# An earlier place for evacuations and a shorter lead for weight splits in the Strassen pairs of a hybrid decoder layer

## The chip, the cores and the metric

The kernel runs on 1 core of one Trainium2 chip. The metric is the device time of one execution in microseconds (us). TensorE (PE) multiplies, VectorE (DVE) and ScalarE (ACT) do elementwise work, GpSimd (POOL) helps them, and SyncE (SP) issues all transfers from one in-order queue. Each engine takes its instructions strictly in the order in which the program lists them.

## The reference

One step of a decoder layer for 512 prompt tokens and 8 x 8 sample tokens (576 columns together), with d_model 2048: a norm, one input projection, sparse attention and a gated recurrence side by side, and the merged output. The part that the change touches is the last line:

```python
m = jax.nn.sigmoid(gm_att) * u_att + jax.nn.sigmoid(gm_rnn) * u_rnn
return x + jnp.einsum('btd,de->bte', m, w_out)      # w_out is 2048 x 2048
```

All of it is float32. The kernel holds each operand of a product as a high part (rounded to the type float32r) and a low part (the rest), and adds three matmuls: high x high, high x low and low x high.

## The kernel before

The program is written as a list of *slots*. A slot is the work of one weight block of 128 x 1024 numbers with 288 columns: 24 matmuls (8 row blocks, three each). The main loop (L1502) walks over the slots and writes, for each, in this order: the high parts that are due, transfers and helpers that were put on this slot (`later`), the low parts that are due, the evacuations of the products that ended in the slot before (`evs`), helpers that were put at the slot's end (`behind`), and then the slot's matmuls. As each engine keeps the order in which its own instructions were written, this sets what stands in front of what on VectorE.

The *weight blocks* are split by `w_high` (L220, on ScalarE, tile whi) and `w_low` (L227, on VectorE, tile wlo = block minus high part). The list `wunits` has the slot in which each split is due. There are three buffers for whi and three for wlo (WHL = 3, L207). A split can thus start only when the product three blocks earlier has read its weights for the last time.

The output projection comes last. Its first four row tiles (kind "y") are plain: four slots each, evacuated by L557. While they run, `y_factors` (L1354) makes the sums of the token factors that the Strassen form needs. The other twelve row tiles are done as six *pairs* (kind "Y") by a Strassen scheme of seven products each instead of eight; a product is one slot. For a pair, four blocks of w_out are loaded (tiles yr, three buffers, and ya, two) and four sums of blocks are made from them on VectorE by `y_sum`: the first s1 = a21 + a22 (L1380), then s2 = s1 - a11 (L1384), a21 = a11 - a21 (L1387) and a11 = a12 - s2 (L1390). The last two write over the block that they read. Blocks of products 0 to 6 are: a11, the fourth sum, a12, the third sum, s2, s1, a22. So the high part of product 1 needs the fourth sum, which needs the second, which needs the first, and the fourth sum may only be made when product 0's block has been split.

The products go to PSUM banks by this table (row operand, column half, bank, whether it begins the bank):

```python
YPROD = ((0, 0, "g", True), (1, 1, "s", True), (1, 0, "g", False), (3, 1, "h", True),
         (2, 1, "t", True), (3, 0, "s2", True), (2, 0, "h", False))
```

Product 2 adds into the bank of product 0, and product 6 into that of product 3; g and h are the two banks of the tag "g". Every product is evacuated when it ends (`y_evac`, L1426: the bank times 0.25 is added to one, two or three pieces of the result tile res, 288, 576 or 864 columns). So product 2 may start only when product 0's evacuation is done, since that one must read product 0 alone.

`y_plan` (L1395) puts a pair's loads and sums on slots. With b the pair's first slot: loads on b-7 and b-6, the last of them (a21) at the end of b-6; sums at the end of b-5, b-4, b-3 and b-3. Splits were due three slots ahead of their product.

Of the kernel before, what the change touches and what calls it, by code (L numbers as in the profile page):

```python
# [114 lines left out]
def nsa_rglru_step(ctx, tc, a, o):  # L115
# [68 lines left out]
    slots, wunits, unit_of = [], [], {}  # L184
    for n, (kind, m, units) in enumerate(tiles):
        base = len(slots)
        if n == 0:
            continue
        if kind[0] == "Y":
            for u in range(7):  # L190
                slots.append((n, 0, u))
                unit_of[n, u] = len(wunits)
                wunits.append((n, u, base - 3 + u))
            continue
        for h in range(2):
            for u in range(len(units)):
                slots.append((n, h, u))
        if n == 1:

            slots += [(n, 1, u) for u in (0, 1, 0, 1)]  # L200
            wunits += [(n, 0, -2), (n, 1, -1)]
            continue
        for u in range(len(units)):
            at = base - 2 if len(units) == 1 else (base - 3 if u == 0 else base - 1)
            wunits.append((n, u, at))
# [75 lines left out]
    def square(c):  # L281

        A.activation(xs[c], xs[c], AF.Square)
        if c:
            V.tensor_add(xs[0], xs[0], xs[c])
        if c == 7:
            V.tensor_add(xsum, xs[0][:, 0], xs[0][:, 1])
# [54 lines left out]
    def at(slot, fn, last=False):  # L342

        (behind if last else later).setdefault(slot, []).append(fn)
# [1024 lines left out]
    def y_load(j, c, par_):  # L1369
        tag, bufs = ("ya", 2) if c and par_ else ("yr", 3)  # L1370
        t = rp_["p"].tile([128, 8, 128], F, tag=tag, name=tag, bufs=bufs)
        S.dma_start(t, a["w_out"][j + c, par_])
        yraw[j, c, par_] = t

    def y_sum(n, j, which):

        a11, a21 = yraw[j, 0, 0], yraw[j, 1, 0]
        if which == 1:
            t = ysum[1] = wp.tile([128, 8, 128], F, tag="raw", name="s1", bufs=WRAW)
            V.tensor_add(t, a21, yraw[j, 1, 1])  # L1380
            units = {0: a11, 2: yraw[j, 0, 1], 5: t, 6: yraw[j, 1, 1]}
        elif which == 2:
            t = ysum[2] = wp.tile([128, 8, 128], F, tag="raw", name="s2", bufs=WRAW)
            V.tensor_sub(t, ysum[1], a11)  # L1384
            units = {4: t}
        elif which == 3:
            V.tensor_sub(a21, a11, a21)  # L1387
            units = {3: a21}
        else:
            V.tensor_sub(a11, yraw[j, 0, 1], ysum[2])  # L1390
            units = {1: a11}
        for u, t in units.items():
            raw[unit_of[n, u]] = t

    def y_plan(n, j):  # L1395
        b = slot_of[n]
        at(b - 7, lambda: y_load(j, 0, 0))
        at(b - 6, lambda: (y_load(j, 0, 1), y_load(j, 1, 1)))
        at(b - 6, lambda: y_load(j, 1, 0), True)
        for which, s in ((1, b - 5), (2, b - 4), (3, b - 3), (4, b - 3)):  # L1400
            at(s, lambda which=which: y_sum(n, j, which), True)

    ybank = {}
# [43 lines left out]
    evs = []  # L1447
# [45 lines left out]
    def sample_work(s):  # L1493
        nonlocal sample_n
        while sample_n is not None and sample_n < (s + 0.5 - sample_from) / (sample_to - sample_from):
            sample_n = next(ssteps, None)
# [5 lines left out]
    for s, (n, h, u) in enumerate(slots):  # L1502
        now[0] = s
        kind, m, units = tiles[n]
        if s == slot_of[first_r]:
            for _ in psteps:
                pass
            for _ in ssteps:
                pass
            for fs in [later.pop(k) for k in sorted(later) if k < s]:  # L1510
                for f in fs:
                    f()
            att.close()
            cqs.close()
            rp_["h"] = ctx.enter_context(tc.tile_pool(name="hp", bufs=1))
            rp_["s"] = ExitStack()
            rp_["p"] = rp_["s"].enter_context(tc.tile_pool(name="rp", bufs=1))
            rnn_begin()
        if s == slot_of[first_u] - 9:
            for k in sorted(k for k in later if k <= s):  # L1520
                for f in later.pop(k):
                    f()
            rp_["s"].close()
            rp_["s"] = ExitStack()
            rp_["p"] = rp_["s"].enter_context(tc.tile_pool(name="up", bufs=1))
            for ct in range(8):
                at(s + 3 * ct // 2, lambda ct=ct: oa_make(ct))
        if s == slot_of[first_y]:
            for e in evs:
                evac(*e)  # L1530
            evs.clear()
            rp_["s"].close()
            rp_["p"] = ctx.enter_context(tc.tile_pool(name="yp", bufs=1))
        ws = []
        while wnext < len(wunits) and wunits[wnext][2] <= s:
            w_high(wnext)
            ws.append(wnext)
            wnext += 1
        for f in scales:
            f()  # L1540
        scales.clear()
        for f in later.pop(s, []):
            f()
        if SQS <= s < SQS + 8:
            at(s, lambda c=s - SQS: square(c), True)
        if NORM - 2 <= s < NORM:
            x_mean(s - NORM + 2)
        if s == NORM:
            x_norm()

        if s < slot_of[first_r]:
            if not prompt_done:
                prompt_done = next(psteps, None) is None and s >= sample_from
                if s >= PG and s not in full:
                    at(s, lambda: next(pages, None), True)
                if prompt_done:
                    sample_from = s + 1
                    ssteps = sample_steps()
                    for _ in pages:
                        pass  # L1560
                    pp["stack"].close()
                    pp["s"] = att.enter_context(tc.tile_pool(name="sp", bufs=1))
            else:
                sample_work(s + 0.5)
        for k in ws:
            w_low(k)
            w_load(lnext)
            lnext += 1
        for n2 in range(n, len(tiles)):
            if slot_of[n2] > s + 3:  # L1570
                break
            name, j = tiles[n2][0][0], tiles[n2][0][-1]
            if name in ("ua", "ur") and "p" in rp_ and s >= slot_of[first_u] - 9 and (name == "ur", j) not in gates_in:
                t = gates_in[name == "ur", j] = rp_["p"].tile([128, NT], F, tag="tgi", name="tgi", bufs=4)
                S.dma_start(t, tg_d[int(name == "ur"), j])
            if name in ("y", "Y") and j not in res_in and s >= slot_of[first_y]:
                j -= j % 2
                res_in[j] = res_in[j + 1] = rp_["p"].tile([128, 2, NT], F, tag="res", name="res", bufs=2)
                S.dma_start(res_in[j], xin[j // 2])
        for e in evs:  # L1580
            evac(*e)
        evs = []
        for f in behind.pop(s, []):
            f()

        if n == 1:
            first_products(s)
            continue
        if kind[0] == "Y":
            y_product(n, kind[1], u)  # L1590
            continue
        wh, wl = whl[n, u]
        last = u == len(units) - 1
        for step, (h2, k) in enumerate([(h, k) for k in range(8)]):
            kk = u * 8 + k
            name = kind[0]
            if kk == 0:
                gbs[h2] = bank("g")
            gb = gbs[h2]
            hs = slice(h2 * HF, h2 * HF + HF)  # L1600
            if step == 4 and ssteps is not None and s < slot_of[first_r]:
                sample_work(s + 1)
            if name == "ua":
                r_h, r_l = oa[kk]
            elif name == "ur":
                r_h, r_l = hr[kk]
            elif name == "y":
                r_h, r_l = mh[2 * k + u], ml[2 * k + u]
            else:
                r_h, r_l = xh[kk], xl[kk]  # L1610
            T.matmul(gb[:, :HF], wh[:, k, :], r_h[:, hs], start=kk == 0, stop=False)  # L1611
            T.matmul(gb[:, :HF], wh[:, k, :], r_l[:, hs], start=False, stop=False)  # L1612
            T.matmul(gb[:, :HF], wl[:, k, :], r_h[:, hs], start=False, stop=last and k == 7)  # L1613
            if last and k == 7:
                evs.append((kind, h2, gb))
# [98 lines left out]
```

## Time and profile before

| what | us |
|---|---|
| median of 3 runs | 1746.25 (1742.62 to 1747.58) |
| profiled execution, its own time | 1744.26 |
| its span in the profile | 1742.5 |
| PE busy | 1688.4 (97%) |
| VectorE busy | 1164.6 (67%) |
| ScalarE busy | 824.6 (47%) |

The span is the time from the first instruction to the last; the execution's own time is 1.76 us longer. A row of a timeline has the start, the duration, the engine, the line, the operation, the output and input tiles, the size, and in brackets how long the engine stood idle before it and what ended that. Matmuls are pipelined: a matmul's row is longer (0.29 us) than the distance to the next one, and the distance is what counts. A row of a table of stretches has the stretch, its length, the busy time and count of PE, of the weight loads, of VectorE, ScalarE and GpSimd, and then the granted clock of PE (1.00 is full), the DMA engines' share and GB/s.

### The profile page before, as it was taken

The numbers are of one execution on the slowest core, as the hardware profiler recorded it, in microseconds if no ns is written. First come the engines' busy times: TensorE is split into PE (matmuls) and PEld (weight loads), VectorE is DVE, ScalarE is ACT, GpSimd is POOL, SyncE is SP. The second block draws the span as 40 slices with busy tenths as digits, with TensorE's granted clock in tenths as the row PEclk, the third lists the DMA queues.
The fourth block names the chain that finished last, engine by engine and source line by source line (L and its number), as shares of the span: only waits on it lengthen the run. The fifth ranks groups of instructions, "written<-read, shape, count | busy, mean of one in ns | idle before, by whom it ended". The sixth has DMA issues, their size and how long they took to land. (4 is left out here: it accounts for less than half of the span.)

```text
span 1742.5 us, 33426 instructions
## 1 busy us (share of the span) xinstructions
PE 1688.4 (97%) x12493; PEld 1656.8 (95%) x12493; DVE 1164.6 (67%) x2398; ACT 824.6 (47%) x1521; POOL 473.8 (27%) x503
## 2 busy tenths in 40 slices
PE   9999999999999999999999999999999999997988
PEld 8999989999999899999999999999999999997988
DVE  6578678768778876468777765667664343485655
ACT  6434544553554454367676663666652121232222
POOL 0025435432533344165455520000022111100000
PEclk9999999999999999999999999999999999998999
DMA  6367435433533443466675753222245445463340
GB/s 218 118 214 239 142 99 175 131 106 120 165 101 117 140 156 126 141 191 203 197 207 180 215 171 99 87 79 91 77 159 196 154 146 166 158 237 111 110 151 28
DMA packets 147460, 257.98 MB, mean 148 GB/s; under 512 B 19937, under 2 KB 80482, under 8 KB 147042
## 3 DMA queue, kind: packets, MB, share of 16 engines
q1 hardware_dynamic: 147298, 255.85, 45.7%
q8 instruction: 98, 1.61, 0.4%
q14 instruction: 64, 0.52, 0.1%
HBM read 228.11 MB, written 36.07 MB: 152 GB/s over the span
## 5 line engine op out<-in xcount | busy, mean ns | idle before, releaser
L1611 PE MATMUL g<-xh,whi 128*128 128x288 f32 x2400 | 719.2, 300 | 0.3 <-DVE gm L499 0.2
L1613 PE MATMUL g<-xh,wlo 128*128 128x288 f32 x2400 | 710.0, 296 | 4.5 <-DVE wlo L230 4.5
L1612 PE MATMUL g<-xl,whi 128*128 128x288 f32 x2400 | 709.4, 296 | 0.0
L1613 PEld LDWEIGHTS g<-xh,wlo 128*128 128x128 f32 x2400 | 452.6, 189 | 5.2 <-DVE wlo L230 5.2
L1611 PEld LDWEIGHTS g<-xh,whi 128*128 128x128 f32 x2400 | 453.2, 189 | 2.5 <-DVE gm L499 0.9
L1612 PEld LDWEIGHTS g<-xl,whi 128*128 128x128 f32 x2400 | 453.2, 189 | 1.3
L230 DVE TENSOR_TENSOR wlo<-raw,whi 128x1024 fp32r<-128x1024 f32 x192 | 256.1, 1334 | 44.5 <-ACT whi L224 44.2
L224 ACT ACTIVATE whi<-raw 128x1024 fp32r<-128x1024 f32 x192 | 201.5, 1050 | 60.8 <-PE g L1612 55.5
L851 POOL TENSOR_TENSOR cr<-cr,wcs 128x512 f32<-128x512 f32 x128 | 178.0, 1396 | 151.9 <-DMA cr<-in_cmp 144.1
L703 ACT ACTIVATE p<-p,sm,rq 128x128 f32<-128x128 f32 (+3 forms) x128 | 82.8, 648 | 144.3 <-DVE sm L700 144.2
L960 POOL TENSOR_TENSOR skl<-kr,skh 128x512 fp32r<-128x512 f32 x80 | 114.2, 1431 | 122.5 <-ACT skh L959 83.2
L711 POOL TENSOR_SCALAR p<-p,sm 128x128 f32<-128x128 f32 (+3 forms) x128 | 68.8, 550 | 220.6 <-DVE sm L708 99.4
L722 DVE TENSOR_TENSOR pt<-t,pt 128x512 fp32r<-128x512 f32 x96 | 66.1, 689 | 63.9 <-ACT pt L721 62.6
L1062 DVE TENSOR_TENSOR sv<-vr,sv 128x256 fp32r<-128x256 f32 (+1 forms) x120 | 77.3, 671 | 17.5 <-ACT sv L1058 17.2
L857 DVE TENSOR_REDUCE skvx<-cr 128x16 f32<-128x512 f32 x128 | 86.6, 676 | 0.4
L552 ACT ACTIVATE mh<-ur 128x288 fp32r<-128x288 f32 x32 | 14.2, 445 | 145.0 <-POOL ur L546 145.0
L1613 PE MATMUL g<-oah,wlo 128*128 128x288 f32 x256 | 75.5, 295 | 0.0
L1613 PE MATMUL g<-hrh,wlo 128*128 128x288 f32 x256 | 75.4, 295 | 0.0
L1612 PE MATMUL g<-oal,whi 128*128 128x288 f32 x256 | 75.4, 295 | 0.0
L1611 PE MATMUL g<-oah,whi 128*128 128x288 f32 x256 | 75.4, 294 | 0.0
L1612 PE MATMUL g<-hrl,whi 128*128 128x288 f32 x256 | 75.3, 294 | 0.0
L1611 PE MATMUL g<-hrh,whi 128*128 128x288 f32 x256 | 75.3, 294 | 0.0
(374 smaller groups left out, 3409.2 us busy)
## 6 DMA issues: line engine op xcount, KB each, us to landing
raw<-in_w_in SPq DMA_DIRECT2D x152, 512.0 KB, 3.4
cr<-in_cmp SPq DMA_DIRECT2D x128, 256.0 KB, 3.6
kr<-in_selk SPq DMA_DIRECT2D x128, 128.0 KB, 3.2
vr<-in_selv SPq DMA_DIRECT2D x128, 128.0 KB, 3.1
tg<-gm SPq DMA_DIRECT2D x32, 288.0 KB, 4.4
tgi<-tg SPq DMA_DIRECT2D x32, 288.0 KB, 4.3
yr<-in_w_out SPq DMA_DIRECT2D x18, 512.0 KB, 4.1
raw<-in_w_rnn SPq DMA_DIRECT2D x16, 512.0 KB, 4.1
```

Source lines behind the costliest of these rows:

```text
L224: A.activation(hi, raw[k], AF.Copy)
L230: V.tensor_sub(lo, raw.pop(k), hi.bitcast(F))
L703: A.activation(p[:, :n], p[:, :n], AF.Exp, bias=sm[:, 1, r - r0:r - r0 + 1], scale=rq[:, i, r:r + 1], accum_out=sm[:, 2, r - r0:r - r0 + 1])
L711: G.tensor_scalar(p[:, :n], p[:, :n], sm[:, 3, r - r0:r - r0 + 1], 1.0, op0=OP.mult, op1=OP.mult)
L722: V.tensor_sub(lo, t, hi.bitcast(F))
L851: G.tensor_tensor(v, v, wcs[:, :, None, :].to_broadcast([128, 4, 4, 32]), op=OP.mult)
L857: V.tensor_reduce(x.kvx[:, :, 8 + n * 4:12 + n * 4], v, axis=AX.X, op=OP.add)
L960: G.tensor_tensor(kl, t, kh.bitcast(F), op=OP.subtract)
L1062: V.tensor_sub(v[:, :, :, 1, :], src, v[:, :, :, 0, :].bitcast(F))
L1611: T.matmul(gb[:, :HF], wh[:, k, :], r_h[:, hs], start=kk == 0, stop=False)
L1612: T.matmul(gb[:, :HF], wh[:, k, :], r_l[:, hs], start=False, stop=False)
L1613: T.matmul(gb[:, :HF], wl[:, k, :], r_h[:, hs], start=False, stop=last and k == 7)
```

## The change

In the pairs, the splits are due two slots ahead of their product instead of three; the sums come at the end of b-4, b-3, b-3 and b-2 instead of b-5, b-4, b-3 and b-3; and in the pairs' slots the evacuations are written in front of the low parts instead of behind them. Nothing is computed otherwise, and the loads stay on their slots.

```diff
@@ the list of splits
-                wunits.append((n, u, base - 3 + u))
+                wunits.append((n, u, base - 2 + u))
@@ y_plan
-        for which, s in ((1, b - 5), (2, b - 4), (3, b - 3), (4, b - 3)):
+        for which, s in ((1, b - 4), (2, b - 3), (3, b - 3), (4, b - 2)):
             at(s, lambda which=which: y_sum(n, j, which), True)
@@ the main loop
+        if kind[0] == "Y":
+            for e in evs:
+                evac(*e)
+            evs.clear()
         for k in ws:
             w_low(k)
             w_load(lnext)
```

VectorE's order in the steady state, before: from product 4's evacuation in one pair (from bank t, 864 columns) to product 1's evacuation in the next (from bank s, 288 columns); wlo from yr, s2 or s1 is the low part of the block named, res from g is an evacuation of bank g or h.

```order
L1426 SCALAR_TENSOR_TENSOR res<-t,res 128x864
L230 TENSOR_TENSOR wlo<-yr,whi 128x1024
L1426 SCALAR_TENSOR_TENSOR res<-s,res 128x2x288
L230 TENSOR_TENSOR wlo<-yr,whi 128x1024
L1426 SCALAR_TENSOR_TENSOR res<-g,res 128x288
L230 TENSOR_TENSOR wlo<-s_20643,whi 128x1024
L1426 SCALAR_TENSOR_TENSOR res<-g,res 128x864
L230 TENSOR_TENSOR wlo<-s_20612,whi 128x1024
L1426 SCALAR_TENSOR_TENSOR res<-s,res 128x288
L1380 TENSOR_TENSOR s_20839<-yr,ya 128x1024
```

The evacuation of product 0 (res from g, 864 columns) has the low part of product 4 (from s_20643, the tile s2) directly in front of it. The same stretch of VectorE after the change:

```order
L1426 SCALAR_TENSOR_TENSOR res<-t,res 128x864
L230 TENSOR_TENSOR wlo<-yr,whi 128x1024
L1390 TENSOR_TENSOR yr<-yr,s_20671 128x1024
L1426 SCALAR_TENSOR_TENSOR res<-s,res 128x2x288
L230 TENSOR_TENSOR wlo<-yr,whi 128x1024
L1426 SCALAR_TENSOR_TENSOR res<-g,res 128x288
L230 TENSOR_TENSOR wlo<-yr,whi 128x1024
L1426 SCALAR_TENSOR_TENSOR res<-g,res 128x864
L230 TENSOR_TENSOR wlo<-yr,whi 128x1024
L1426 SCALAR_TENSOR_TENSOR res<-s,res 128x288
L230 TENSOR_TENSOR wlo<-s_20671,whi 128x1024
```

In front of the evacuation of product 0 now stands the low part of product 2 (from yr), and product 4's low part comes after product 1's evacuation. The fourth sum (L1390) stands behind the low part of product 0's block. At the entry into the pairs, VectorE's difference from the last factors (L1366) to the first low parts of the first pair (lines with - are before, with + after):

```order
 L1366 TENSOR_TENSOR tl<-yo,th 128x576
-L230 TENSOR_TENSOR wlo<-yr,whi 128x1024
+L1384 TENSOR_TENSOR s_19767<-s_19725,yr 128x1024
 L1387 TENSOR_TENSOR yr<-yr 128x1024
-L1390 TENSOR_TENSOR yr<-yr,s_19727 128x1024
 L230 TENSOR_TENSOR wlo<-yr,whi 128x1024
 L557 SCALAR_TENSOR_TENSOR res<-g,res 128x288
-L230 TENSOR_TENSOR wlo<-yr,whi 128x1024 x2
+L1390 TENSOR_TENSOR yr<-yr,s_19767 128x1024
+L230 TENSOR_TENSOR wlo<-yr,whi 128x1024
 L557 SCALAR_TENSOR_TENSOR res<-g,res 128x288
```

The first evacuation in this piece (L557, the last plain tile's first half) stood behind the low parts of products 0 and 1 and the fourth sum; it now stands behind the low part of product 0 alone. The first sum (L1380), ahead of this piece, moved from before the last but one set of factors to behind it.

## The prediction

> **What bounds the kernel now.** I read the page first, then TensorE's waits, then a table of stretches over the end of the run, then the timelines of TensorE, VectorE and ScalarE in one pair.
>
> ```profile
> span 1742.5 us, 33426 instructions
> PE 1688.4 (97%) x12493; PEld 1656.8 (95%) x12493; DVE 1164.6 (67%) x2398; ACT 824.6 (47%) x1521; POOL 473.8 (27%) x503
> ```
>
> TensorE (PE) is busy for 97% of the span; everything else has room. So only time in which PE stands still, or runs slowly, can be won. PE's waits from 1300 us to the end (total, times, longest):
>
> ```profile
> PE g L1417 <- DVE res L1426: 20.0, 6, 3.3
> PE g L1417 <- DVE res L557: 4.5, 1, 4.5
> PE g L1611 <- DVE res L557: 1.3, 1, 1.3
> ```
>
> Six waits of 3.3 us, one for each Strassen pair, and one of 4.5 us at the first product: each time the first matmul of a product (L1417) waits until VectorE has evacuated a bank (L1426, L557). The table of stretches has the length, PE's busy time and count, then the other engines, the granted clock and the DMA:
>
> ```profile
> 1526.00:1568.80 42.80, 41.53 (x313) 41.20 (x311) 37.64 (x63) 16.67 (x22) 0.00 (x0) 1.00 0.67 232
> 1568.80:1585.40 16.60, 8.79 (x50) 8.45 (x48) 8.20 (x9) 4.12 (x4) 0.00 (x0) 0.78 0.45 151
> 1639.74:1666.99 27.25, 23.91 (x169) 23.71 (x169) 17.18 (x18) 7.42 (x7) 0.00 (x0) 0.94 0.34 113
> 1694.25:1721.53 27.28, 23.95 (x168) 23.74 (x169) 17.18 (x18) 7.42 (x7) 0.00 (x0) 0.94 0.18 65
> ```
>
> A pair takes 27.25 us, and the clock in it is 0.94, not the 1.00 of the stretch before. PE's timeline around one wait shows why:
>
> ```profile
> 1633.04 0.30 PE L1417 MATMUL s<-mh,whi 128*128 128x288 f32 x1
> ...
> 1636.11 0.29 PE L1419 MATMUL s<-mh,wlo 128*128 128x288 f32 x1
> 1639.74 0.58 PE L1417 MATMUL g<-mh,whi 128*128 128x288 f32 x1 [3.33 <-DVE res L1426]
> 1640.11 0.44 PE L1418 MATMUL g<-ml,whi 128*128 128x288 f32 x1
> 1640.35 0.44 PE L1419 MATMUL g<-mh,wlo 128*128 128x288 f32 x1
> ```
>
> Product 1's 24 matmuls start from 1633.04 to 1636.11: 23 steps of 0.1335 us, so a product takes 3.20 us. After the wait the step is 0.24 us: a wait costs its length and then a stretch at near half speed. Of 27.25 us, 7 x 3.20 = 22.4 are work, 3.33 waiting, and the remaining 1.5 the slow start.
>
> Now who is late. VectorE's and ScalarE's timelines in the same pair (product 0 ends and product 1 starts at 1633.04, product 1 ends at 1636.24):
>
> ```profile
> 1627.48 1.23 DVE L1390 TENSOR_TENSOR yr<-yr,s 128x1024 f32<-128x1024 f32 x1
> 1631.06 1.05 DVE L1426 SCALAR_TENSOR_TENSOR res<-t,res 128x864 f32<-128x864 f32 x1
> 1633.16 0.75 DVE L1426 SCALAR_TENSOR_TENSOR res<-s,res 128x576 f32<-128x576 f32 x1
> 1635.41 0.45 DVE L1426 SCALAR_TENSOR_TENSOR res<-g,res 128x288 f32<-128x288 f32 x1
> 1637.40 1.23 DVE L230 TENSOR_TENSOR wlo<-s,whi 128x1024 fp32r<-128x1024 f32 x1 [1.54 <-ACT whi L224]
> 1638.54 1.05 DVE L1426 SCALAR_TENSOR_TENSOR res<-g,res 128x864 f32<-128x864 f32 x1
> ```
>
> ```profile
> 1633.17 1.06 ACT L224 ACTIVATE whi<-yr 128x1024 fp32r<-128x1024 f32 x1 [2.11 <-PE g L1418]
> 1636.31 1.06 ACT L224 ACTIVATE whi<-s 128x1024 fp32r<-128x1024 f32 x1 [2.08 <-PE s L1418]
> ```
>
> Product 2 adds into product 0's bank, so it needs product 0's evacuation. That could begin at about 1633.2 but begins at 1638.54, because the low part of product 4 (1637.40) stands in front of it on VectorE. That low part waits for its high part (1636.31), and this waits for product 1 to give back one of three weight buffers. The chain is end of product 1, +1.06, +1.23, +1.05, then PE: 3.33 us with the hops. With three buffers a lead of three products is a lead in name only: the buffer comes free when the product itself has ended.
>
> **The change, part by part.** No instruction is added or removed on a path; the evacuations, splits and sums keep their durations: low part and sum 1.23, evacuations 0.45, 0.75 or 1.05, high part 1.06. ScalarE has 7.4 us of work in a pair.
>
> *Steady state.* Let Tk be the start of product k if PE never waits, 3.20 apart; a prime marks the next pair. At Tk the bank of product k-1 is ready and its weight buffer free. High parts then run Tk+0.1 to +1.15. Following VectorE's new order with the durations above:
> T3: evacuation 2 to +0.55, low 5 from 1.2 to 2.4, first sum to 3.65.
> T4: evacuation 3 from 0.45 to 0.9, low 6 to 2.45, second and third sums to 4.9.
> T5: evacuation 4 from 1.7 to 2.75, low 0' to 4.0, fourth sum to 5.2.
> T6: evacuation 5 from 2.0 to 2.75; high 1', which needs the fourth sum, to 3.15; low 1' to 4.4.
> T0': evacuation 6 from 1.2 to 1.65, low 2' to 2.9.
> T1': evacuation 0' to 1.15, low 3' to 2.45: the backlog is gone.
> PE's needs: product 2' needs evacuation 0' at T1'+1.15 and starts at T1'+3.2, 2.05 to spare. Product 0' needs low 0' at T5+4.0, starts at T5+6.4: 2.4 to spare. Product 1' needs low 1' at T6+4.4: 2.0 to spare. Product 2' needs low 2' 3.5 before its start. The wait goes, and nothing is late in its place; the slow start goes with it. The cover is these 2 us; without it each pair pays what is missing and again 1.5.
>
> *Loads.* SyncE's queue keeps its order, but its releases move: the fourth weight block of the next pair waits for low 3, done at T1+2.45. The landing times of these loads (tile yr):
>
> ```profile
> DMA to landing us min/median/max: 3.2/4.1/5.6
> ```
>
> So it is there by T3+1.7 at worst, and the first sum asks for it at T3+2.4. From that sum to low 1' VectorE and ScalarE need 11.4 us, and product 1' starts at T3+16.0: PE would first feel a load of over 8.5 us. The other blocks are freed by low 1 and low 2 and issued earlier. The pair from 1639.74 moved 113 GB/s over 27.25 us; the same bytes in 22.4 us are 137, where the stretch from 1526 moved 232.
>
> *Entry.* The 4.5 us wait at the first product, and VectorE in front of it:
>
> ```profile
> 1568.64 0.29 PE L1613 MATMUL g<-mh,wlo 128*128 128x288 f32 x1
> 1573.47 0.58 PE L1417 MATMUL g<-mh,whi 128*128 128x288 f32 x1 [4.53 <-DVE res L557]
> ...
> 1577.93 0.34 PE L1417 MATMUL g<-mh,whi 128*128 128x288 f32 x1
> ```
>
> ```profile
> 1553.21 1.22 DVE L230 TENSOR_TENSOR wlo<-raw,whi 128x1024 fp32r<-128x1024 f32 x1
> 1557.27 1.23 DVE L1380 TENSOR_TENSOR s<-yr,ya 128x1024 f32<-128x1024 f32 x1 [2.84 <-DMA yr<-in_w_out]
> 1558.41 0.45 DVE L1358 TENSOR_TENSOR ye<-ye 128x288 f32<-128x288 f32 x1
> ...
> 1561.77 0.45 DVE L557 SCALAR_TENSOR_TENSOR res<-g,res 128x288 f32<-128x288 f32 x1
> 1562.14 1.22 DVE L1384 TENSOR_TENSOR s<-s,yr 128x1024 f32<-128x1024 f32 x1
> ...
> 1571.73 1.22 DVE L230 TENSOR_TENSOR wlo<-yr,whi 128x1024 fp32r<-128x1024 f32 x1 [1.20 <-ACT whi L224]
> 1572.87 0.45 DVE L557 SCALAR_TENSOR_TENSOR res<-g,res 128x288 f32<-128x288 f32 x1
> ```
>
> VectorE sat 2.84 us waiting for a load, with the factors (L1358 on) behind it, and later stood at low 1, which waits for a high part that waits for the fourth sum, with the evacuation behind. In the new order the factors (3.4 us, 1558.41 to 1561.77) fill the hole, if their own loads are in, from 1554.4 to 1557.8. Then evacuation to 1558.2, first sum to 1559.4 (its load is there at 1557.2), second factors to 1562.8, two sums to 1565.3, low 0 to 1566.5, evacuation to 1566.9, fourth sum to 1568.2, high 1 to 1569.3, low 1 to 1570.6. Product 0 is due at 1568.77 with 1.9 to spare, product 1 at 1571.97 with 1.4.
>
> *Sum.* The end, from the chain that ended last:
>
> ```profile
> 1738.99 0.14 PE g L1419
> 1739.16 0.46 DVE res L1426
> ```
>
> The 42 products now take from 1568.77 (1568.64 and one step) to 1739.13, 170.4 us. Without waits: 42 x 3.20 = 134.4. Saving 36.0: 24.5 of waits (20.0 + 4.5) and 11.5 of slow clock. What follows the last matmul is unchanged. The profiled execution took 1744.26, so 1708.3; the median of the runs is 2.0 higher, which gives 1710.3. I take 1709.
>
> The Trainium skill, page "TensorE: Matmul & The Clock Gate", section "Wait — 56ns, not 53.3ns?", puts the warm step at columns over 2.4 GHz and 2.5 ns, here 122.5 ns, and the cold one at columns over 1.2 GHz, 240 ns. The trace has the cold step (0.24) but 0.1335 for the warm one; by the page's figure the products would take 123.5 us and the estimate would be 1697; I keep to the row.
>
> **The rivals.**
> *A, the bank is the limit.* If two g banks were simply too few for a product that adds into a bank still being emptied, the wait would stay, at 1744 to 1746. Against it: the evacuation began 5.3 us after its bank was ready. For it: the change adds no bank and no buffer. The Trainium skill, page "Perfetto Trace Analysis", section "Optimization Strategy" under "Identifying Performance Opportunities", says that a gap repeating on the engine that should be saturated can mean too little SBUF or PSUM; by that this one would stay.
> *B, slower: the fourth block comes late.* Past 8.5 us from issue to landing PE waits at product 1' for the excess, and pays 1.5 of slow clock, in five pairs. At 14.2 us that is 36, the whole gain; at 16 us it is 5 x 9.0 = 45, so 1753. For it: loads and stores come 18% closer together. Against it: 5.6 is the longest landing in tile yr.
> *C, VectorE slips.* It is busy 17.18 us of what would be 22.4, 77%, and all in one queue. A slip of 3 us from the third sum on, 1 more than the spare, costs 1 + 1.5 in five pairs: 1721. Against it: 88% from 1526 to 1568.8 (37.64 of 42.80) cost PE 1.3.
> *D, the entry stays.* If the factors' loads come later than 1554.4, or the first sum's does, the entry keeps its wait: 4.5 and, at 0.107 lost for each of the 18 slow matmuls from 1573.47 to 1577.93, 1.9: 1714.7. For it: the spare there is the smallest of all.
>
> **How the numbers follow.** The forecast 0.83, D 0.07, C 0.05, A 0.03, B 0.02. The three runs lie from 1.6 below to 3.3 above the profiled time, so the forecast alone spans 1706.7 to 1711.6; with 1.5 below for the step and D with its scatter above, the range is 1705 to 1717, which leaves out C, A and B, a tenth. A difference of 0.3%, 5 us, is about what a measurement of this kernel can tell from none. Forecast, D and C are faster by more: 0.95; A is the same: 0.03; B slower: 0.02.
>
> **What would show it.** Right: no wait of PE for L1426, pairs of 22.4 us at clock 1.00, the evacuation of product 0 within 0.3 us of its end, no wait before the first product, a last matmul near 1703. Wrong: PE waiting for wlo or whi (C); VectorE's first sum waiting for a load (B); a wait of over 3 us near 1569 (D); pairs still at 27 (A).

## The result, and the profile after

The changed kernel took 1704.5 us (median of 4 runs, 1704.15 to 1705.82) beside 1745.88 for the kernel before (median of 4): a ratio of 0.9767, with a 95% interval of 0.9750 to 0.9783. A second set of 5 runs gave 1704.88 (1704.27 to 1706.92) beside 1744.7, ratio 0.9776 (0.9763 to 0.9790). The profiled execution took 1704.21, with a span of 1702.4. So the kernel is some 40 us faster, 4 more than forecast, and the first median lies half a microsecond below the stated range.

The head of the page, then the table of stretches (stretch, length, busy time and count of PE, weight loads, VectorE, ScalarE and GpSimd, PE's clock, DMA share, GB/s):

```profile
span 1702.4 us, 33396 instructions
PE 1672.3 (98%) x12493; PEld 1642.3 (96%) x12493; DVE 1159.6 (68%) x2398; ACT 824.5 (48%) x1521; POOL 475.2 (28%) x503
```

```profile
1526.00:1565.46 39.46, 39.46 (x299) 39.46 (x299) 37.40 (x62) 16.30 (x22) 0.00 (x0) 1.00 0.67 236
1613.10:1635.34 22.24, 22.24 (x170) 22.24 (x169) 17.34 (x18) 7.43 (x7) 0.00 (x0) 1.00 0.43 149
```

A pair is now 22.24 us instead of 27.25, at clock 1.00 instead of 0.94, with PE busy in all of it: 7 products of 3.18 us and nothing else. From 1500 us to the end the view of PE's waits has no row at all. The engines' counts of working instructions are the same (the total, which counts others too, is 30 smaller), and VectorE has the same work in a pair, 17.2 us before and 17.3 now, packed into 22.24.

VectorE's timeline in the third pair's first products (product 1 starts at 1613.10, product 2 at 1616.30, by PE's timeline):

```profile
1604.99 1.05 DVE L1426 SCALAR_TENSOR_TENSOR res<-t,res 128x864 f32<-128x864 f32 x1
1605.96 1.22 DVE L230 TENSOR_TENSOR wlo<-yr,whi 128x1024 fp32r<-128x1024 f32 x1
1607.21 1.23 DVE L1390 TENSOR_TENSOR yr<-yr,s 128x1024 f32<-128x1024 f32 x1
1608.35 0.75 DVE L1426 SCALAR_TENSOR_TENSOR res<-s,res 128x576 f32<-128x576 f32 x1
1609.64 1.23 DVE L230 TENSOR_TENSOR wlo<-yr,whi 128x1024 fp32r<-128x1024 f32 x1 [0.54 <-ACT whi L224]
1610.79 0.45 DVE L1426 SCALAR_TENSOR_TENSOR res<-g,res 128x288 f32<-128x288 f32 x1
1611.15 1.22 DVE L230 TENSOR_TENSOR wlo<-yr,whi 128x1024 fp32r<-128x1024 f32 x1
1613.30 1.06 DVE L1426 SCALAR_TENSOR_TENSOR res<-g,res 128x864 f32<-128x864 f32 x1 [0.92 <-PE g L1419]
1614.32 1.22 DVE L230 TENSOR_TENSOR wlo<-yr,whi 128x1024 fp32r<-128x1024 f32 x1
```

```profile
1613.10 0.29 PE L1417 MATMUL s<-mh,whi 128*128 128x288 f32 x1
...
1616.30 0.29 PE L1417 MATMUL g<-mh,whi 128*128 128x288 f32 x1
```

The evacuation of product 0 (864 columns from bank g, at 1613.30) waits for PE now, not PE for it. It starts 0.2 us after product 0's end and is done at 1614.36 (1613.30 + 1.06), 1.94 us ahead of product 2. The low parts of products 0 and 1 end at 1607.18 and 1610.87, 2.7 and 2.2 us ahead of their products.

The entry, on VectorE (L557 evacuates plain tiles, L1380 is the first sum, L230 at 1567.26 the low part of product 1) and on PE:

```profile
1556.20 0.45 DVE L557 SCALAR_TENSOR_TENSOR res<-g,res 128x288 f32<-128x288 f32 x1
1556.57 1.21 DVE L1380 TENSOR_TENSOR s<-yr,ya 128x1024 f32<-128x1024 f32 x1
...
1563.33 1.22 DVE L230 TENSOR_TENSOR wlo<-yr,whi 128x1024 fp32r<-128x1024 f32 x1
1564.47 0.45 DVE L557 SCALAR_TENSOR_TENSOR res<-g,res 128x288 f32<-128x288 f32 x1
...
1567.26 1.23 DVE L230 TENSOR_TENSOR wlo<-yr,whi 128x1024 fp32r<-128x1024 f32 x1 [1.21 <-ACT whi L224]
```

```profile
1565.33 0.30 PE L1617 MATMUL g<-mh,wlo 128*128 128x288 f32 x1
1565.46 0.29 PE L1417 MATMUL g<-mh,whi 128*128 128x288 f32 x1
```

The first product follows the last plain tile without a gap. The evacuation it needs is done at 1564.92, 0.5 us ahead of it: the tightest place of the changed kernel. The first sum no longer waits for its load, and the evacuation L557 that stood behind it, at 1561.77 before, now starts at 1556.20.

### The profile page after: what moved, and what is told of

The parts are those of the page before. It is cut to its first block, busy times and chain, and to the rows that moved or that the text cites. A ratio compares the mean times of both kernels' runs of the same rounds, so it can differ in the third digit from the quotient of the medians.

```text
span 1702.4 us, 33396 instructions
## 1 busy us (share of the span) xinstructions
PE 1672.3 (98%) x12493; PEld 1642.3 (96%) x12493; DVE 1159.6 (68%) x2398; ACT 824.5 (48%) x1521; POOL 475.2 (28%) x503
## 5 line engine op out<-in xcount | busy, mean ns | idle before, releaser
L1615 PE MATMUL g<-xh,whi 128*128 128x288 f32 x2400 | 717.9, 299 | 0.1
L1615 PEld LDWEIGHTS g<-xh,whi 128*128 128x128 f32 x2400 | 451.8, 188 | 1.6 <-ACT c L405 0.3
L230 DVE TENSOR_TENSOR wlo<-raw,whi 128x1024 fp32r<-128x1024 f32 x192 | 253.9, 1322 | 44.2 <-ACT whi L224 43.9
L1062 DVE TENSOR_TENSOR sv<-vr,sv 128x256 fp32r<-128x256 f32 (+1 forms) x120 | 77.3, 672 | 17.4 <-ACT sv L1058 17.2
L1615 PE MATMUL g<-oah,whi 128*128 128x288 f32 x256 | 75.5, 295 | 0.0
L1615 PE MATMUL g<-hrh,whi 128*128 128x288 f32 x256 | 75.4, 294 | 0.0
```

What stands on the lines that cost most here:

```text
L230: V.tensor_sub(lo, raw.pop(k), hi.bitcast(F))
L1062: V.tensor_sub(v[:, :, :, 1, :], src, v[:, :, :, 0, :].bitcast(F))
```

## The experiments

The theory to be tested: PE waits for evacuation 0 because VectorE's queue has a low part in front of it that needs the end of a later product; the slow clock after a wait of 3.3 us costs half as much again; the sums' slots and the loads have to fit behind that. The rivals: one part of the change carries all; the slow steps are not the clock; the loads have far more room, or none.

**Evacuations in front alone.** The kernel before with

```diff
+        if kind[0] == "Y":
+            for e in evs:
+                evac(*e)
+            evs.clear()
         for k in ws:
             w_low(k)
```

> Only the evacuations move in front of the low parts in the pairs' slots; lead three and the sums' slots stay as before. VectorE then still has low 3 directly in front of evacuation 0 (low 3 is written one slot earlier), and low 3 needs the end of product 0: high from 0.13 to 1.19 us after it, low to 2.4, evacuation to 3.42, PE at 3.57, where product 2 is due at 3.2. Theory (what counts is which product's end the instruction in front of the evacuation waits for): waits of about 0.4 us a pair for evacuation 0 in place of 3.33, too short for the slow clock, and the entry keeps its 4.5 us and 1.9 of slow clock, since the plain tiles' evacuations are not moved: 1704.5 + 6.4 + 6 x 0.4 = about 1713. Rival 1 (any wait is followed by the slow clock, 1.5 us): about 1722. Rival 2 (the shorter lead does it, the place of the evacuation does nothing): no change from before, 1746.

Measured: 1716.05 us (1714.08 to 1717.56), ratio 0.9835 (0.9822 to 0.9849). PE's waits from 1300 us on:

```profile
PE g L1417 <- DVE res L557: 4.5, 1, 4.5
PE g L1615 <- DVE res L557: 1.7, 1, 1.7
PE g L1417 <- DVE res L1426: 1.2, 6, 0.2
```

The added code moves later lines down by four, so L1615 is the L1611 of before. VectorE at one of the six waits has the low part of product 3 directly in front of evacuation 0:

```profile
1603.25 1.23 DVE L230 TENSOR_TENSOR wlo<-yr,whi 128x1024 fp32r<-128x1024 f32 x1 [1.32 <-ACT whi L224]
1604.39 1.05 DVE L1426 SCALAR_TENSOR_TENSOR res<-g,res 128x864 f32<-128x864 f32 x1
```

The six waits are 0.2 us each. From start to start a wait costs 0.4 us: the two steps at it are 0.50 and 0.21 us instead of 0.13 each. So pairs take 22.7 us (1605.59 to 1628.25 to 1650.93 between the starts of product 2), 0.4 over the 22.24 of the change. That is the forecast of the theory; rival 1 (each wait pays 1.5 more) and rival 2 fall. The entry's 4.5 us stay, as expected. The total is 3 us above the expectation; the wait of 1.7 us in the plain tiles is part of it, and it had not been put down to the sums (below).

**Shorter lead and later sums alone.** The change without the four lines above.

> Lead two and the sums one slot later as in the change, but the evacuations stay behind the low parts. Low 3 again stands directly in front of evacuation 0, so the theory gives the same 0.4 us a pair, and no wait at the entry, where the lead and the sums did the work: 1704.5 + 6 x 0.4 = about 1707. Rival 1 (slow clock after any wait): about 1716. Rival 2 (the lead alone decides): 1704.5, as with the whole change. Rival 3 (the place of the evacuation decides alone): 1740 or more.

Measured: 1708.35 us (1707.89 to 1710.67), ratio 0.9796 (0.9782 to 0.9809). PE's waits:

```profile
PE g L1417 <- DVE res L1426: 1.5, 6, 0.5
PE g L1417 <- DVE res L557: 1.1, 1, 1.1
PE g L1611 <- DVE res L557: 0.5, 1, 0.5
```

Again 0.2 us in each of five pairs and 0.5 in the first, periods of 22.68; rivals 2 and 3 fall, as the time is neither 1704.5 nor 1740. The wait of 1.1 us at the entry was not expected. The order there is that of the change, but in this execution the first sum waited 1.40 us for its load:

```profile
1560.29 1.23 DVE L1380 TENSOR_TENSOR s<-yr,ya 128x1024 f32<-128x1024 f32 x1 [1.40 <-DMA yr<-in_w_out]
```

That is more than the 0.5 us that the changed kernel had to spare there, so the entry's gain hangs on when this load lands.

So the lead and the place of the evacuation are two ways to the same order on VectorE: each alone moves the low part of product 4 from in front of evacuation 0 and leaves low 3, one product earlier. The two together take away low 3 as well. The entry needs the lead and the sums, which the first experiment lacked: with them 1.1 us of its 4.5 are left here, and none in the change.

**First and second sum on their old slots.** The change with

```diff
-        for which, s in ((1, b - 4), (2, b - 3), (3, b - 3), (4, b - 2)):
+        for which, s in ((1, b - 5), (2, b - 4), (3, b - 3), (4, b - 2)):
```

> The change with the first and second sums back on the slots of before (the fourth must stay, since it writes over product 0's block, and the third stays as it was). Theory: in the steady state the first sum waits up to some 1.5 us for its load with nothing urgent behind it, so PE waits nowhere; at the entry VectorE waits 2.8 us for that load in front of the factors, so evacuation and low 0 come about 1 us too late for product 0: 1705 to 1706. Rival (the sums' slots carry the gain at the entry): the wait of 4.5 us there and its slow clock are back, 1711.

Measured: 1711.3 us (1709.12 to 1714.21), ratio 0.9807 (0.9793 to 0.9820); the expectation was 5 to 6 us too low. PE's waits, and VectorE at one of the first sums:

```profile
PE s L1419 <- DVE wlo L230: 1.6, 3, 0.8
PE g L1615 <- DVE res L557: 1.3, 1, 1.3
PE g L1417 <- DVE res L557: 0.6, 1, 0.6
```

```profile
1586.39 1.23 DVE L1380 TENSOR_TENSOR s<-yr,ya 128x1024 f32<-128x1024 f32 x1 [5.66 <-DMA yr<-in_w_out]
1587.54 0.45 DVE L1426 SCALAR_TENSOR_TENSOR res<-g,res 128x288 f32<-128x288 f32 x1
1587.90 1.22 DVE L230 TENSOR_TENSOR wlo<-s,whi 128x1024 fp32r<-128x1024 f32 x1
```

A slot earlier the sum waits 4.5 to 5.7 us for its load in the five pairs after the first, and the low part of product 5 stands behind it, which I had overlooked: product 5 waits for it up to 0.8 us. The 1.3 us in the plain tiles are back as well, and 0.6 at the entry. The total is that of the rival, but not by its mechanism: at the entry 0.6 us are back and not 4.5. In the profiles, from the beginning of the plain tiles to the last matmul, this kernel took 6 us more than the change, 2.3 of them up to the first product and 3.6 in the pairs. So the later sums are worth several microseconds by themselves, in the steady state too.

**The waits filled.** The kernel before with matmuls that write to a free bank and whose result nobody reads:

```diff
+        fills = 25 if u == 2 else 34 if u == 0 and n == first_Y else 0
+        if fills:
+            ib = bank("m")
+            for _ in range(fills):
+                T.matmul(ib[:, :HF], mh[0][:, :128], mh[0][:, HS[0]], start=True, stop=True)
         for i in range(8):
```

> The kernel before, with 25 extra matmuls of 288 columns into a free bank ahead of product 2 in each pair and 34 ahead of the first product, whose result nobody reads: they fill waits of 3.33 and 4.5 us without shortening them. Theory (11.5 of the 36 us are the slow clock after waits): the steps after the wait stay at 0.133 us and the time falls by about 11.5 to 1734, though PE has more to do. Rival (the slow steps come from something else, such as other engines' traffic at that moment): the steps stay at 0.24 and the time stays at 1746 or rises.

Measured: 1733.57 us (1732.01 to 1735.62) beside 1744.39, ratio 0.9940 (0.9926 to 0.9953): 10.8 us faster for 184 matmuls more. The table of stretches, over one whole stretch of 27 us in the pairs, and PE's timeline at one fill:

```profile
1585.00:1612.00 27.00, 26.95 (x204) 26.75 (x204) 17.19 (x18) 7.92 (x8) 0.00 (x0) 1.00 0.34 108
```

```profile
1630.53 3.46 PE L1419 MATMUL m<-mh 128*128 128x288 f32 x25
```

The clock is 1.00, and the pairs last 25.82 us (1630.53 to 1656.35 between fills) instead of 27.25. The evacuation is as late as it was, 2.3 us after product 1's end in both. So the slow steps are the clock, they follow from PE's idleness, and they cost the 11.5 us of the prediction's sum, or nearly.

**Part of the wait filled.** The same with 6 and 15 extra matmuls.

> The kernel before with only 6 extra matmuls ahead of product 2 and 15 ahead of the first product (nobody reads their result): PE still stands idle for about 2.5 us at a time. Waits up to 1.65 us left the step at 0.133 us, waits of 3.3 us were followed by 0.24. If the slow clock needs more than 2.5 us of idleness: no slow steps, about 1734 as with all 25. If 2.5 us are enough: slow steps after each wait, 1744.

Measured: one run, 1745.83 us beside 1745.43. PE's timeline at the first pair's product 2 (the added code moves lines down by five):

```profile
1584.99 0.58 PE L1422 MATMUL g<-mh,whi 128*128 128x288 f32 x1 [2.54 <-DVE res L1431]
1585.37 0.44 PE L1423 MATMUL g<-ml,whi 128*128 128x288 f32 x1
1585.61 0.44 PE L1424 MATMUL g<-mh,wlo 128*128 128x288 f32 x1
```

Idle for 2.54 us is enough for steps of 0.24. In the other five pairs the wait is 2.54 us too, and there the slow steps come only after some ten steps of 0.13, about 1.5 us behind the wait. In the same run a wait of 1.88 us in the plain tiles was followed by slow steps too, and one of 1.04 at the entry was not.

**A lead of one product.** The change with

```diff
-                wunits.append((n, u, base - 2 + u))
+                wunits.append((n, u, base - 1 + u))
...
-        for which, s in ((1, b - 4), (2, b - 3), (3, b - 3), (4, b - 2)):
+        for which, s in ((1, b - 4), (2, b - 3), (3, b - 3), (4, b - 1)):
```

> The change with a lead of one product and the fourth sum at the end of the last slot ahead of the pair, where the shorter lead forces it. Theory (a split needs 2.4 us after the buffer or the evacuation, a product lasts 3.2, and the sums of slots 3 to 6 push 1.7 us of backlog onto it): the blocks' buffers come back a slot later, the fourth block's load lands near the start of slot 4, and the low parts of products 5, 6, 0 and 1 are up to a few us late: 1 to 4 us of waiting in each of five pairs, 1710 to 1725, in waits for wlo and not for evacuations. Rival (a split is short against a product, so any lead of one or more is enough): 1705.

Measured: 1711.65 us (1709.16 to 1712.58), ratio 0.9808 (0.9794 to 0.9821). PE's waits:

```profile
PE g L1419 <- DVE wlo L230: 4.0, 5, 1.1
```

Five waits of 0.5 to 1.1 us, at the third matmul of product 6 in the pairs ahead of another. In front of low 6 VectorE has three sums, and the first of them waited 1.5 to 2.3 us for its load, as the expectation had it; which part of the lateness is the load's and which the sums' was not separated. A lead of two products covers the backlog, a lead of one does not, and one of three is only two.

**A late fourth block.** The change with the load of a21 issued twice in the pairs after the first, into the same tile:

```diff
         S.dma_start(t, a["w_out"][j + c, par_])
+        if c and not par_ and j > YSTD:
+            S.dma_start(t, a["w_out"][j + c, par_])
```

> The change with the fourth block (a21) of pairs 2 to 6 loaded twice, the second load written over the first, so that it lands about 4.6 us later, some 9 to 11.5 us after the first issue. The prediction's walk says that PE first feels a landing of over 8.5 us: waits of 1 to 3 us in each of five pairs, for wlo or whi of products 6, 0 or 1, 1709 to 1720. Rival (the load has far more room): no wait, 1705.

Measured: 1716.3 us (1712.94 to 1717.81), ratio 0.9835 (0.9821 to 0.9848). PE's waits, and VectorE's first sum (lines are two further down; the first of the two loads was issued at 1574.15):

```profile
PE g L1421 <- DVE wlo L230: 5.3, 7, 0.9
PE s L1421 <- DVE wlo L230: 1.3, 5, 0.3
PE g L1419 <- DVE res L1428: 0.2, 1, 0.2
```

```profile
1584.32 1.22 DVE L1382 TENSOR_TENSOR s<-yr,ya 128x1024 f32<-128x1024 f32 x1 [4.38 <-DMA yr<-in_w_out]
```

This block is there 10.2 us after its first issue and makes products 0 and 1 of the next pair wait 0.76 and 0.26 us for their low parts. The five blocks compared (a block is there when the first sum starts; the loss is that of all steps over 0.13 us in the products that wait for it):

| pair | there after (us) | by the walk, over 8.5 | PE lost |
|---|---|---|---|
| 2 | 10.2 | 1.7 | 1.6 |
| 3 | 9.4 | 0.9 | 1.6 |
| 4 | 10.3 | 1.8 | 2.5 |
| 5 | 10.9 | 2.4 | 3.0 |
| 6 | 9.8 | 1.3 | 2.0 |

The order of size is right, and in four of five pairs the loss is 0.7 us more than the walk gives. In the walk the load is issued 2.45 us after product 1 starts. Here it was issued 2.9 us after it for pair 2 and 3.8 for the others (product 1's start reckoned back from its third matmul), because low 3, for which it waits, was itself pushed back. So a late block makes the next one late as well. That the first pair agrees is in part luck: its load was issued 0.5 us later than in the walk, which would give 2.2.

**Scatter of the beginning.** The changed kernel and the kernel before, each profiled twice more, for the point where the plain tiles begin.

> The changed kernel itself once more, for its scatter. The profile before reached the plain output tiles at 1516.4 us, that of the change at 1514.6, and the first paid 1.3 us there for a late load of the result tile; nothing that was changed stands ahead of that point, and the other four kernels lie from 1515.6 to 1518.6. If that is chance: plain tiles begin anywhere from 1514 to 1519, the pairs again take 133.6 us, the median is 1704 to 1709. If the change itself made the earlier part shorter: 1704.5 again, with the plain tiles at 1514.6.

> The kernel before itself, for a second profile: six waits of 3.3 us and one of 4.5, pairs of 27.2 us, and a start of the plain tiles between 1514 and 1519 us, if that point scatters by chance.

> The changed kernel a third time, for the point where its plain tiles begin: 1514.6 us in both profiles so far, against 1515.6 to 1518.6 in eight profiles of kernels that are the same up to there. Chance: anywhere from 1514 to 1519. Not chance: 1514.6 again.

> The kernel before a third time, for the same point: 1516.4 and 1516.3 so far. Chance: anywhere from 1514 to 1519. Not chance: 1516.3 again.

Measured: the change 1704.88 (5 runs) and 1706.77 (one), the kernel before 1745.21 and 1742.23 (one each). In the profiles the plain tiles of the change begin at 1514.6, 1514.6 and 1517.2 us, those of the kernel before at 1516.4, 1516.3 and 1515.3, and those of the other kernels at 1515.6 to 1518.6. In the third pair of profiles the change was the later one, so nothing ties this point to the change: it scatters within 4 us. From there to the first product the change took 50.9 us in all three. The 1.3 us that an expectation lays to a late load of the result tile are the wait behind the first sum (next section). The wait in the plain tiles was there in all three profiles of the kernel before, in the third with slow steps behind it:

```profile
1561.89 0.41 PE L1611 MATMUL g<-mh,whi 128*128 128x288 f32 x1 [1.96 <-DVE res L557]
1562.13 0.30 PE L1612 MATMUL g<-ml,whi 128*128 128x288 f32 x1
1562.27 0.37 PE L1613 MATMUL g<-mh,wlo 128*128 128x288 f32 x1
1562.43 0.44 PE L1611 MATMUL g<-mh,whi 128*128 128x288 f32 x1
```

The same profile has a wait of 3.33 us, the first pair's, with no slow steps behind it:

```profile
1584.32 0.37 PE L1417 MATMUL g<-mh,whi 128*128 128x288 f32 x1 [3.33 <-DVE res L1426]
1584.53 0.29 PE L1418 MATMUL g<-ml,whi 128*128 128x288 f32 x1
1584.66 0.29 PE L1419 MATMUL g<-mh,wlo 128*128 128x288 f32 x1
```

The clock stays at 1.00 there, and the stretch to the next such wait takes 25.81 us, against 27.35 and a clock of 0.94 for the one after it. So the same wait does not always bring the clock down; the other 17 of these waits in the three profiles did.

No experiment points to a version that beats the change: in its pairs PE has neither a wait nor a slow step left. A fourth weight buffer under the old order was not tried; whether it would have helped as well stays open.

## Why the prediction was right

The mechanism was right in the main, the order on VectorE and the slow clock, and the sum was 4 us short: 0.8 in the pairs, 1.5 in a wait that it left standing, and 1.8 by chance. From one profiled execution to the other 40.05 us were saved (1744.26 to 1704.21):

| where | forecast | measured |
|---|---|---|
| pairs: first product to last matmul's end | 36.0 (170.4 to 134.4) | 36.8 (170.4 to 133.6) |
| plain tiles (52.4 to 50.9) | 0 | 1.5 |
| ahead of the plain tiles, the same instructions (1516.4 to 1514.6) | 0 | 1.8, chance |

*The bound.* Six waits and their slow starts were the gain, and all of it came: 22.24 us a pair, where 22.4 was forecast from a step of 0.1335 us; the step is 0.1324.

*The slow clock* as a term of its own (11.5 us) was right: filling the waits gained 10.8. What the prediction did not know is that the two parts can be had apart: a wait of 0.2 us pays no slow clock, so either half of the change alone already wins nearly all in the pairs (22.7 us each).

*The walk through VectorE's order* held. Forecast spares: 2.05, 2.4 and 2.0 us for evacuation 0, low 0 and low 1; measured 1.94, 2.7 and 2.2. Its bound for the fourth block was tested with blocks that came after 9.4 to 10.9 us: forecast 8.1 us in five pairs, measured 10.6. The walk left out that a late block delays the next one's load.

*The loads' worst landing* was wrong: 5.6 us in the profile before, 6.8 in the one after (median 4.6 for 4.1). The other two profiles of each kernel agree, 5.5 and 5.6 before and 6.5 after. That the same bytes move in less time is the likely cause, but it was not tested by itself. The rate in a pair came to 149 GB/s and not 137: the 113 of the prediction's row is for a stretch from product 2 to product 2, and from product 1 to product 1 the kernel before moved 121. The first sum did wait twice, 1.62 and 0.20 us, and nothing was lost, as the walk's bound is 8.5. Rival B was thus nearer than the 0.02 suggests: the room is 1.7 us over the longest landing seen, and blocks that come after some 10 us cost about 11 us in all, far from the 36 that would make the kernel as slow as before.

*The entry* came out as forecast in the three profiles of the change, but with 0.5 us to spare and not 1.9. The difference is the step that failed: I left the plain tiles' wait of 1.3 us where it was and used it as evidence of how little VectorE's load matters there. But the first sum's wait of 2.84 us and the evacuation at 1561.77 were in the prediction's own rows; PE's second half of the last plain tile waited for just that evacuation, from 1561.0 to 1562.28. With the first sum a slot later this wait goes too, 1.5 us from start to start, and PE reaches the entry 1.5 us sooner. With so little to spare one late load brings part of the entry's wait back, as in the run with the shorter lead and later sums alone. Every profile with the first sum a slot later lacks this wait at the last plain tile; every one with it in its old place, five kernels, has 1.0 to 2.0 us there.

*Rival A* (too few banks) is refuted: the banks and buffers are the same and the gap is gone. By the page "Perfetto Trace Analysis" of the Trainium skill (section "Optimization Strategy") a repeating gap can mean too little memory; here it meant the order of one queue. *C* and *D* did not happen in the change. The lead of one shows C in the small, and the early sums and the shorter lead alone show D (0.6 and 1.1 us).

The range's low end had 1.5 us for the step and nothing for an unseen gain; the measured medians, 1704.5 and 1704.88, lie just below it. Its high end leaves out a microsecond of its own sum: D's 1714.7 and the 3.3 of scatter make 1718. The forecast was taken 0.7 above the profiled sum of 1708.3, towards the median; without that it would have been 3.8 off instead of 4.5.

## What to carry to other kernels

When an engine waits for something short that could have run long ago, look at what stands directly in front of that thing on its in-order queue, and whose end that one needs: a lead in the source is only as long as the buffers behind it. For an order that is moved, walk the new order through one whole period with measured durations and write down the spare at each place where the busy engine needs something; then look for every other wait that hangs on the moved instructions, upstream too. And a wait on TensorE can have two prices, its length and a slow stretch behind it. Here waits of 0.2 us cost 0.4 and waits of 3.33 cost about 5 in a pair, so a wait that is made short enough saves more than its length; filling it down to 2.54 us was not enough.

## What the runs showed of the hardware

TensorE's step for 288 columns is 0.132 to 0.133 us at clock 1.00, and 0.24 in the slow stretches, which ended 2.8 to 6.1 us after the wait. From 1500 us on no wait of up to 1.65 us was followed by slow steps. Waits of 1.88, 1.96, 2.54, 3.00, 3.33 and 4.53 us were, at once or, after five of those of 2.54, some 1.5 us later; but one of 3.33 was not. So the length of a wait alone does not decide it, and what does stays open. The Trainium skill, page "TensorE: Matmul & The Clock Gate", section "What's actually happening", has the clock drop after an idle window of about 3.4 us; these traces show it after waits little over half as long. Loads of 512 KB landed in 4.1 us (median) where a pair, from product 1 to product 1, moved 121 GB/s, and in 4.6 where it moved 149, with the longest going from 5.6 to 6.8.
